# A state-space mixer's recurrence, from eight-step blocks to one scan instruction in a rotating frame

## The chip, the cores and the metric

The kernel runs on one core of one Trainium2 chip. The metric is the device time of one execution in microseconds (us). Engines are named as in the profile: PE (TensorE matmul), PEld (its weight load), DVE (VectorE), ACT (ScalarE), POOL (GpSimd) and SP (SyncE); a "q" behind a name is that engine's instruction queue (ACTq issues DMAs, for example). L1440 is line 1440 of the kernel before.

## What is computed

The program is two transformer-like blocks for one sequence of 256 tokens of width 1024 and a context of 256 tokens, all in float32. The part that the change touches is the state-space mixer of the second block's second layer. For each of two directions d, 64 groups and 64 states it runs a diagonal complex recurrence over the tokens:

```
step = exp(log_step);  mag = exp(lam_re * step)
a    = mag * (cos(lam_im * step) + i * sin(lam_im * step))
h_t  = a * h_(t-1) + B u_t          (h and B complex, u real)
y_t  = Re(C h_t) + D u_t
```

It runs first over the context (only its last state is kept), then over the latent sequence, which starts from that last state. The backward direction runs from the last token to the first.

## The kernel before, in words

**Chunks of four tokens.** Tables made once turn four tokens into one chunk: `ssm_build` (L1177) computes `a` from the parameters, then matrices that inject a chunk's four inputs into the state (tensor `ssm_m`), read a chunk's four outputs from the state (`ssm_g`), and hold the direct path inside a chunk (`ssm_t`); all go to DRAM. So 256 tokens are 64 chunks, and the recurrence over chunks has the factor a^4. States lie on 128 partitions; each partition holds 32 "pairs" x 2 directions x (real, imaginary) x 64 chunks.

**The recurrence before** is done in blocks of 8 chunks. `ssm_local` (L1425) walks the 8 places of a block, all blocks at once: for each of 7 steps two products of the previous place with a^4 (L1440) and two sums (L1443), each instruction over half of 8 pairs, 128 elements per partition. One call covers 8 pairs, so four calls cover the context and four the latent sequence; of each four, group g = 1 runs on GpSimd (`SSM_POOL`, `CTX_POOL`), the others on VectorE. `ssm_carry` (L1456 to L1464) then runs over the 8 blocks with a^32, four instructions of 128 elements for each of 7 steps. In the latent part `ssm_apply` (L1467 to L1481) adds the carried state, times a table of powers of a^4 (`spw`, from DRAM), to every place of every block: five instructions for each of 8 quarters q and each direction, most of the backward ones on GpSimd.

**The order of the stage.** `ssm_ctx` (L1484) normalises the context, multiplies it by the input weights (L1508), injects (L1408), runs the blocks and leaves `last`. It is called inside the dense expert layer ahead of it (`peer_dense`, L1049), so its instructions lie between those of that layer's last blocks (matmuls L777, splits L308 and L315). `ssm_mixer` (L1535) then normalises x, multiplies (lines 335 to 338), transposes into `suT`, injects all 32 pairs, runs blocks and carries, calls `fill` (modulation matmuls L796 to L806, weights `ada_w_t`), and goes q by q through apply, readout matmuls (L1596 with `ssm_t`, L1598 with `ssm_g`) and a Gelu (L1599). After that y is transposed and split (L1615, L1616) and the output matmuls follow.

**What sets the order.** The kernel is written in a framework that orders each engine's instructions by its own estimate of times; a lower priority (`c.low()`) is given to `ssm_build` and to the sparse expert branch. On the chip every engine and queue runs its list in that fixed order. Tiles come from pools with a number of buffers (`bufs`); a write to a buffer waits for the last reader of what was there. The weights `w` (1 MB tiles, L64) all go through one pool of 5 buffers and SP's queue, in program order. `ssm_build`'s tiles lie in the pool `sb`; when it is closed, the pools of the sparse branch and of the next norm take its space (L1672 to L1690), so these wait for `ssm_build`'s last store.

Of the kernel before, what the change touches and what calls it, by code (L numbers as in the profile page):

```python
# [41 lines left out]
SSM_POOL = (1,)  # L42
CTX_POOL = (1,)
APPLY_V = (0,)
# [1132 lines left out]
def ssm_build(c, pool, sb):  # L1177

    nc, I, tc = c.nc, c.I, c.tc
    A1, A2, B1, B2 = (pool.tile([P, 32, 2, 2], F32, name=n) for n in ("A1", "A2", "B1", "B2"))  # L1180
    pd = c.dram.tile([P, 1024], F32, name="ssm_p")
# [51 lines left out]
    pw = sb.tile([P, 5, 2, W], F32, name="pw")  # L1233
    tt(pw[:, 1, 0], mag, hs, ALU.mult)
    tt(pw[:, 1, 1], mag, sn, ALU.mult)
    ar, ai = pw[:, 1, 0], pw[:, 1, 1]
# [17 lines left out]
    def cmul(ore, oim, xr, xi, yr, yi, w1, w2):  # L1254
        tt(w1, xr, yr, ALU.mult)
        tt(w2, xi, yi, ALU.mult)
        tt(ore, w1, w2, ALU.subtract)
        tt(w1, xr, yi, ALU.mult)
        tt(w2, xi, yr, ALU.mult)
        tt(oim, w1, w2, ALU.add)  # L1260

    for n in (2, 3, 4):
        cmul(pw[:, n, 0], pw[:, n, 1], pw[:, n - 1, 0], pw[:, n - 1, 1], ar, ai, t1, t2)

    pt = sb.tile([P, 32, 2, 2, 8], F32, name="pt")
    nc.gpsimd.memset(pt[:, :, :, :, 0:1], 0.0)
    cur = pw[:, 4]
    for n in range(1, 9):
        if n > 1:
            nx = sb.tile([P, 2, W], F32, tag="pn", name="pn", bufs=2)  # L1270
            cmul(nx[:, 0], nx[:, 1], cur[:, 0], cur[:, 1], pw[:, 4, 0], pw[:, 4, 1], t1, t2)
            cur = nx
        srcs = [cur[:, j].rearrange("p (d q) -> p q d", d=2) for j in range(2)]
        if n < 8:
            for j in range(2):
                nc.scalar.copy(pt[:, :, :, j, n], srcs[j])
        if n in (1, 8):
            X1, X2 = (A1, A2) if n == 1 else (B1, B2)
            for r in range(2):
                nc.scalar.copy(X1[:, :, :, r], srcs[0])  # L1280
                nc.scalar.mul(X2[:, :, :, r], srcs[1], 1.0 - 2.0 * r)
    nc.scalar.dma_start(pd, pt.rearrange("p a d r n -> p (a d r n)"))
# [114 lines left out]
    return dict(a4=(A1, A2), a32=(B1, B2), powers=pd, m=md, g=gd, t=td)  # L1397


def ssm_inject(c, uT, Sx, mats, g, first=0):  # L1400


    for q in range(4 * g, 4 * g + 4):
        m = mats(q).rearrange("p (a j m) -> p a j m", a=2, j=4)
        ps = c.ps()
        for a in range(2):
            for j in range(4):
                c.nc.tensor.matmul(  # L1408
                    ps[:, (a * 4 + j) * 64 : (a * 4 + j + 1) * 64], m[:, a, j, :], uT[:, 2 * q + a, :], start=True, stop=True
                )  # L1410
        i = 2 * q - first
        c.evac(Sx[:, i : i + 2].rearrange("p a d r j -> p (a d r j)"), ps, eng="a")
# [12 lines left out]
def ssm_local(c, eng, pool, A, Sx, p0, n, tag, first=0):  # L1425

    m = n // 2

    def at(h, j):
        return _view(Sx, (p0 - first + h * m) * 256 + j, [[256, m], [128 + 7 - 2 * j, 2], [64, 2], [8, 8]])

    def step(j, i):

        for h in range(2):
            a = [v[:, p0 + h * m : p0 + (h + 1) * m].unsqueeze(4).to_broadcast([P, m, 2, 2, 8]) for v in A]
            if i < 2:
                t[h][i] = pool.tile([P, m, 2, 2, 8], F32, tag=f"{tag}{i}{h}", name=f"sl{i}", bufs=1)
                eng.tensor_tensor(t[h][i], a[i], at(h, j - 1), ALU.mult)  # L1440
            else:
                v = t[h][0] if i == 2 else _view(t[h][1], 8, [[32, m], [16, 2], [-8, 2], [1, 8]])
                eng.tensor_tensor(at(h, j), at(h, j), v, ALU.add)  # L1443

    t = [[None, None], [None, None]]
    for j in range(1, 8):
        for i in range(4):
            step(j, i)


def block_view(t, s):

    return _view(t, s, [[32, 32], [16 + 7 - 2 * s, 2], [8, 2]])


def ssm_carry(c, pool, B, e, before, after):  # L1456

    nc = c.nc
    t1 = pool.tile([P, 32, 2, 2], F32, tag="st1", name="st1")
    t2 = pool.tile([P, 32, 2, 2], F32, tag="st2", name="st2")  # L1460
# [6 lines left out]
def ssm_apply(eng, pool, pw, C, Sx, H, p0, n, d, tag):  # L1467

    shp = [P, n, 2, 8, 7]
    ps = slice(p0, p0 + n)  # L1470
    t1 = pool.tile(shp, F32, tag=tag + "1", name="sa1", bufs=1)
    t2 = pool.tile(shp, F32, tag=tag + "2", name="sa2", bufs=1)
    cb = C[:, ps, d].rearrange("p q r b -> p q (r b)").unsqueeze(3).to_broadcast([P, n, 16, 7])
    for r, t in enumerate((t1, t2)):
        power = _view(pw, p0 * 32 + d * 16 + r * 8 + (1 if d == 0 else 7), [[32, n], [0, 16], [1 - 2 * d, 7]])
        eng.tensor_tensor(t.rearrange("p q r b j -> p q (r b) j"), cb, power, ALU.mult)
# [443 lines left out]
```

## Time and profile before

| what | us |
|---|---|
| median of 3 runs | 3650.92 (3642.49 to 3659.8) |
| the profiled execution's own time | 3635.85 |
| its span | 3634.1 |
| PE busy | 3284.0 (90%) |
| DVE busy | 2640.1 (73%) |
| ACT busy | 1402.9 (39%) |
| POOL busy | 1338.2 (37%) |

The span runs from the first to the last instruction; the profiled execution's own time is 1.75 us longer. Busy shares are averages over stages with different limits, so the stages have to be looked at one by one. The state-space stage lies at 2445 to 2683 us; the set-up with `ssm_build` at 0 to 342 us. A duration of an instruction reaches a little into the next one on its engine, so a sum of durations can be larger than the time they took.

### The profile page before, as it was taken

The page shows a single profiled execution, that of the slowest core. Times are in us where ns is not written, and L with a number is a line of the kernel's source. Part 1 is how long each engine was busy: PE and PEld are TensorE (multiplying, and loading weights), DVE is VectorE, ACT ScalarE, POOL GpSimd, SP SyncE. Part 2 cuts the span into 40 slices and gives each one's busy share as a digit, 9 for nine tenths or more (in the row PEclk, how much of TensorE's full clock was granted, in tenths as well). Part 3 has the DMA queues.
Part 4 walks back from the last instruction along what each step waited for, and adds up shares of the span by engine and source line. Part 5 has one row for each costly group of instructions (what it writes and reads, how often), then busy time and mean ns, then how long its engine had stood idle before and what let it go on. Part 6 is the DMA issues. An engine that isn't in the chain of part 4 may idle for free.

```text
span 3634.1 us, 49746 instructions
## 1 busy us (share of the span) xinstructions
PE 3284.0 (90%) x18136; PEld 2665.8 (73%) x18136; DVE 2640.1 (73%) x5276; ACT 1402.9 (39%) x2586; POOL 1338.2 (37%) x1021
## 2 busy tenths in 40 slices
PE   6996987999889988879999999997589999999998
PEld 4775563747437756678899999976477988999987
DVE  5676986555655568878988888859968987555555
ACT  3553222011310023237444544442133475544454
POOL 0000244444334447448544444414444374001000
PEclk9997998999899999999999999998799999999999
DMA  8875778899588988586998888853554466555553
GB/s 304 288 246 185 280 254 312 336 343 338 211 315 333 355 325 277 178 275 206 357 342 329 338 335 330 336 197 109 199 197 174 163 192 238 209 209 209 209 203 116
DMA packets 280485, 940.44 MB, mean 259 GB/s; under 512 B 22944, under 2 KB 136880, under 8 KB 209200
## 3 DMA queue, kind: packets, MB, share of 16 engines
q1 hardware_dynamic: 142560, 608.22, 46.0%
q0 software_dynamic: 77184, 281.05, 21.2%
q10 hardware_dynamic: 60496, 47.99, 4.0%
q8 instruction: 142, 2.33, 0.2%
q14 instruction: 103, 0.84, 0.1%
HBM read 870.60 MB, written 66.58 MB: 258 GB/s over the span
## 4 chain that ended last, share of the span: by engine, by line
PE 57%; DVE 21%; DMA 13%; issue 4%; POOL 3%; ACT 2%; ACTq 1%; DVEq 0%; POOLq 0%; SPq 0%
PE bank L777 18%; PE bank L350 6%; PE bank L349 6%; PE bank L348 6%; DMA gat<-peer_u_rows,idx 5%; DMA gat<-peer_v_rows,idx 5%; PE bank L364 4%; PE bank L357 4%; DVE spl L315 2%; DVE sl L1440 2%; PE bank L909 2%; POOL o L1102 2%; PE bank L1105 1%; PE bank L337 1%; PE bank L335 1%
## 5 line engine op out<-in xcount | busy, mean ns | idle before, releaser
L315 DVE TENSOR_TENSOR spl<-w,sph 128x1024 fp32r<-128x1024 f32 x552 | 701.9, 1273 | 344.0 <-ACT sph L308 341.8
L308 ACT CAST sph<-w 128x1024 fp32r<-128x1024 f32 x632 | 661.9, 1049 | 558.9 <-PE bank L349 372.6
L350 PE MATMUL bank<-hs,spl 128*128 128x256 f32 x2048 | 582.5, 284 | 6.7 <-DVE spl L315 6.7
L348 PE MATMUL bank<-hs,sph 128*128 128x256 f32 x2048 | 581.0, 284 | 2.0 <-DVE mod L806 1.8
L349 PE MATMUL bank<-hs,sph 128*128 128x256 f32 x2048 | 581.0, 284 | 0.0
L1015 DVE CUSTOM_DVE_ANT_0 gat<-gat,htok 128x1024 f32<-128x1024 f32 x256 | 331.7, 1303 | 177.5 <-DMA gat<-peer_u_rows,idx 154.9
L1027 DVE SCALAR_TENSOR_TENSOR pacc<-gat,act,pacc 128x1024 f32<-128x1024 f32 x256 | 333.8, 1304 | 149.9 <-DMA gat<-peer_v_rows,idx 134.4
L348 PEld LDWEIGHTS bank<-hs,sph 128*128 128x128 f32 x2048 | 392.5, 192 | 11.6 <-ACT sph L308 1.9
L350 PEld LDWEIGHTS bank<-hs,spl 128*128 128x128 f32 x2048 | 392.7, 192 | 10.5 <-DVE spl L315 9.3
L349 PEld LDWEIGHTS bank<-hs,sph 128*128 128x128 f32 x2048 | 392.6, 192 | 8.3 <-issue 0.5
L315 POOL TENSOR_TENSOR spl<-w,sph 128x1024 fp32r<-128x1024 f32 x80 | 201.4, 2518 | 453.5 <-ACT sph L308 436.3
L364 PE MATMUL bank<-hT,w 128*128 128x256 f32 x1472 | 328.6, 384 | 14.1 <-DVE cv L509 8.4
L364 PEld LDWEIGHTS bank<-hT,w 128*128 128x128 f32 x1472 | 283.3, 193 | 64.9 <-issue 11.6
L777 PE MATMUL bank<-sph,wsl 128*128 128x512 f32 x1024 | 318.6, 392 | 2.3 <-DVE wsl L315 2.2
L1000 POOL DMA_INDIRECT gat<-peer_v_rows,idx x176 | 214.2, 1217 | 286.5 <-PE bank L357 61.2
L777 PE MATMUL bank<-spl,wsh 128*128 128x512 f32 x1024 | 319.4, 393 | 0.1
L777 PE MATMUL bank<-sph,wsh 128*128 128x512 f32 x1024 | 307.5, 394 | 2.4 <-ACT wsh L308 2.4
L1000 POOL DMA_INDIRECT gat<-peer_u_rows,idx x176 | 219.1, 1245 | 227.5 <-DVE act L1015 77.9
L357 PE MATMUL bank<-w,hT 128*128 128x512 f32 x576 | 255.6, 603 | 2.2 <-ACT sg L432 2.2
L777 PEld LDWEIGHTS bank<-sph,wsl 128*128 128x128 f32 x1024 | 192.2, 188 | 45.3 <-DVE wsl L315 2.6
L777 PEld LDWEIGHTS bank<-spl,wsh 128*128 128x128 f32 x1024 | 189.8, 188 | 39.8 <-DVE spl L315 0.3
L357 PEld LDWEIGHTS bank<-w,hT 128*128 128x128 f32 x576 | 110.7, 194 | 135.9 <-issue 132.0
(444 smaller groups left out, 5730.3 us busy)
## 6 DMA issues: line engine op xcount, KB each, us to landing
w<-peer_u_t SPq DMA_DIRECT2D x128, 1024.0 KB, 5.6
w<-peer_v_t SPq DMA_DIRECT2D x128, 1024.0 KB, 5.1
w<-ada_w_t SPq DMA_DIRECT2D x48, 1024.0 KB, 6.7
w<-wq_t SPq DMA_DIRECT2D x32, 1024.0 KB, 5.4
w<-w_in_t SPq DMA_DIRECT2D x32, 1024.0 KB, 7.9
gspill<-gstg SPq DMA_DIRECT2D x32, 896.0 KB, 4.6
gq<-gspill SPq DMA_DIRECT2D x28, 1024.0 KB, 6.2
w<-wqk SPq DMA_DIRECT2D x24, 1024.0 KB, 5.3
```

Source lines behind the costliest of these rows:

```text
L308: nc.scalar.copy(hi, src)
L315: eng.tensor_tensor(lo, src, hi.bitcast(F32), ALU.subtract)
L348: mm(ps, wh[:, ks], hh[:, k, :], start=k == 0, stop=False)
L349: mm(ps, wh[:, ks], hl[:, k, :], start=False, stop=False)
L350: mm(ps, wl[:, ks], hh[:, k, :], start=False, stop=k == KD - 1)
L357: m = self.nc.tensor.matmul(outs[t], hT[:, k, t * P : (t + 1) * P], w[k], start=k == 0, stop=k == KD - 1)
L364: m = self.nc.tensor.matmul(ps, block[:, k * P : (k + 1) * P], hT[:, k, :], start=k == 0, stop=k == KD - 1)
L777: c.nc.tensor.matmul(acc[t][cc], a[:, ts_], b[:, cc * 512 : (cc + 1) * 512], start=first and j == 0, stop=last and j == 2,)
L909: nc.tensor.matmul(ps[:, b * P : (b + 1) * P], wv[:, kt, k * P : (k + 1) * P], ks[:, kt, :], start=kt == 0, stop=kt == 1,)
L1000: g = nc.gpsimd.indirect_dma_start(out=gt, out_offset=None, in_=tab, in_offset=bass.IndirectOffsetOnAxis(ap=idx[:, t, s : s + 1], axis=0))
L1015: use = nc.vector.tensor_tensor_reduce(out=gt, in0=gt, in1=h[:, t, :], scale=1.0, scalar=0.0, op0=ALU.mult, op1=ALU.add, accum_out=act[:, ...
L1027: use = nc.vector.scalar_tensor_tensor(acc, gt, act[:, t, s : s + 1], acc, ALU.mult, ALU.add)
```

## The change

The state is turned by the phase of a^4: with a^4 = m e^(i theta), the turned state e^(-i n theta) h_n obeys a recurrence with the real factor m, which VectorE's `tensor_tensor_scan` runs over all chunks of several pairs in one instruction, separately for the real and the imaginary part. A decay table `dec` holds m everywhere and 0 at each pair's first chunk, so that one scan goes over 4 or 8 pairs. Afterwards the state is turned back.

- `ssm_build`: the powers of a up to a^32 (L1254 to L1282: 60 instructions of 64 elements on VectorE, 22 copies on ACT, one store) go. In their place come a normalisation of (cos, sin), a squaring chain on GpSimd (7 times 5 instructions of 64 elements), m and a^4 for all pairs, and 8 phase tables of 4 pairs each, on GpSimd: 2 memsets and 6 doubling levels of 6 instructions, with 8, 16, 32, 64, 128 and 256 elements. Each table (512 KB) is stored to DRAM by a DMA on ACT's queue; the table's buffer is single.
- `ssm_ctx`: eight steps of 4 pairs in place of four of 8. Each injects, loads its phase table (GpSimd's queue, 2 buffers), makes `dec` (two ACT copies, one GpSimd memset, one buffer), turns, scans, and copies the last chunk and its phase out (ACT); the turning back is done once at the end for the last chunk alone. The buffers of the injection weights `cw` go from 4 to 3.
- `ssm_mixer`: four groups of 8 pairs. Groups 0 to 2 are injected first, then `fill` follows, then group by group: phase tables (two DMAs on ACT's queue, 2 buffers), turn, add the start state, scan, turn back into `H` (2 buffers), and readout of two q. Group 3 is injected inside group 0's turn, when its buffer comes free; its weights are then asked for after `ada_w_t` and `ssm_t`. The apply and the carries go. GpSimd has no arithmetic left here.

The diff, cut to its core:

```diff
-SSM_POOL = (1,)
-CTX_POOL = (1,)
-APPLY_V = (0,)
...
 def ssm_build(c, pool, sb):
...
-    for n in (2, 3, 4):
-        cmul(pw[:, n, 0], pw[:, n, 1], pw[:, n - 1, 0], pw[:, n - 1, 1], ar, ai, t1, t2)
...
+    square(lv[:, 1], hs, sn)
+    square(lv[:, 0], lv[:, 1, 0], lv[:, 1, 1])
+    for l in range(1, 6):
+        square(lv[:, l], lv[:, l - 1, 0], lv[:, l - 1, 1])
...
+    def phases(k):
...
+        for l in range(6):
+            L = 1 << l
+            src = [_view(ph, cs * 512, [[320 - L, 2], [64, 4], [1, L]]) for cs in range(2)]
+            dst = [_view(ph, cs * 512 + L, [[320 - 3 * L, 2], [64, 4], [1, L]]) for cs in range(2)]
+            m = [_view(lv, l * 2 * W + cs * W + 4 * k, [[32, 2], [1, 4], [0, L]]) for cs in range(2)]
+            wv = w[:, :, :, :L]
+            for cs in range(2):
+                gp.tensor_tensor(dst[cs], src[0], m[cs], ALU.mult)
+                gp.tensor_tensor(wv, src[1], m[1 - cs], ALU.mult)
+                gp.tensor_tensor(dst[cs], dst[cs], wv, ALU.add if cs else ALU.subtract)
+        nc.scalar.dma_start(pd[k], ph.rearrange("p s d a n -> p (s d a n)"))
...
+def ssm_decay(c, pool, m4, p0, n):
+
+    dec = pool.tile([P, 2, n, 64], F32, tag="dec", name="dec")
+    for d in range(2):
+        c.nc.scalar.copy(dec[:, d], m4[:, p0 : p0 + n, d].unsqueeze(2).to_broadcast([P, n, 64]))
+    c.nc.gpsimd.memset(_view(dec, 0, [[n * 64 + 63, 2], [64, n]]), 0.0)
+    return dec
+
+
+def ssm_turn(nc, pool, ph, S, n):
+
+    w1, w2 = (pool.tile([P, 2, 2, n * 64], F32, tag=f"sw{i}", name=f"sw{i}") for i in range(2))
+    cs, si = (_view(ph, i * n * 128, [[n * 64, 2], [0, 2], [1, n * 64]]) for i in range(2))
+    nc.vector.tensor_tensor(w1, S.rearrange("p d r a j -> p d r (a j)"), cs, ALU.mult)
+    nc.vector.tensor_tensor(w2, _view(S, n * 64, [[n * 128, 2], [-n * 64, 2], [1, n * 64]]), si, ALU.mult)
+    return w1, w2
+
+
+def ssm_scan(c, pool, ph, dec, S, n, ini=None):
...
+    w1, w2 = ssm_turn(nc, pool, ph, S, n)
+    flat = S.rearrange("p d r a j -> p d r (a j)")
+    for r in range(2):
+        nc.vector.tensor_tensor(flat[:, :, r], w1[:, :, r], w2[:, :, r], ALU.subtract if r else ALU.add)
+    if ini is not None:
+        o = edge(S, n, False)
+        nc.vector.tensor_tensor(o, o, ini.rearrange("p a d r -> p d r a"), ALU.add)
+    N = n * 64
+    for d in range(2):
+        for r in range(2):
+            s = _view(S, (d * 2 + r) * N + d * (N - 1), [[1 - 2 * d, N]])
+            f = _view(dec, d * N + d * (N - 1), [[1 - 2 * d, N]])
+            nc.vector.tensor_tensor_scan(s, f, s, 0.0, ALU.mult, ALU.add)
...
 def ssm_mixer(c, mats, modT, x, last, fill, gate):
...
+            Sg = {g: inject(g) for g in range(3)}
+            fill(sy)
...
+            for g in range(4):
+                gs = slice(8 * g, 8 * g + 8)
+                ph = sy.tile([P, 4, 8, 64], F32, tag="ph", name="ph", bufs=2)
+                for h in range(2):
+                    nc.scalar.dma_start(
+                        ph[:, :, 4 * h : 4 * h + 4], mats["phase"][2 * g + h].rearrange("p (s a n) -> p s a n", s=4, a=4)
+                    )
+                S_ = Sg.pop(g)
+                ssm_scan(c, sy, ph, ssm_decay(c, sy, mats["m4"], 8 * g, 8), S_, 8, ini[:, gs])
+
+                w1, w2 = ssm_turn(nc, sy, ph, S_, 8)
+                if g == 0:
+                    Sg[3] = inject(3)
+                H = sy.tile([P, 2, 2, 8, 64], F32, tag="Hx", name="Hx", bufs=2)
+                nc.scalar.copy(edge(H, 8, False), last[:, gs].rearrange("p a d r -> p d r a"))
                 for d in range(2):
...
+                    for r in range(2):
+                        o, i = (slice(1, 64), slice(0, 63)) if d == 0 else (slice(0, 63), slice(1, 64))
+                        v1, v2 = (w[:, d, r].rearrange("p (a j) -> p a j", a=8)[:, :, i] for w in (w1, w2))
+                        nc.vector.tensor_tensor(H[:, d, r, :, o], v1, v2, ALU.add if r else ALU.subtract)
+                for q in (2 * g, 2 * g + 1):
...
```

## Rows read from the trace of the kernel before

**Rows 1.** Stretches of the span: us, busy time (count) by engine, clock, DMA share, GB/s

```profile
core 0: us, PE busy (x) PEld busy (x) DVE busy (x) ACT busy (x) POOL busy (x), PEclk, DMA share, GB/s
0.00:342.00 342.00, 263.15 (x1618) 208.92 (x1618) 223.02 (x631) 164.61 (x439) 8.54 (x15) 0.91 0.78 272
2445.00:2683.00 238.00, 164.47 (x1161) 143.71 (x1161) 222.74 (x484) 52.59 (x86) 126.35 (x161) 0.84 0.46 165
```

**Rows 2.** Chain of work, 2445 to 2683 us: shares of the 238 us by line

```profile
by line: DVE sl L1440 28.0%; DVE cSx L1443 14.6%; DVE Sx L1443 13.3%; DVE sa L1476 7.7%; PE bank L1598 4.5%; DVE spl L315 4.0%; DVE sa L1477 3.0%; DVE Hx L1481 2.8%; DVE sa L1478 2.3%; issue 2.2%; DVE st L1461 1.9%; DVE st L1463 1.8%; DVE s
```

**Rows 3.** Chain of work in order of time, 2440 to 2690 us: start us, us, what

```profile
2449.10 0.73 DVE sl L1440 x2
...
2583.21 2.30 DVE sl L1440 x4
...
2603.48 1.18 DVE sl L1440 x4
...
2667.64 0.97 DVE Hx L1481
2668.66 1.09 PE bank L1598 x8
...
2680.88 0.87 PE bank L1598 x8
...
2683.15 2.18 DVE y L1616 x4
```

**Rows 4.** DVE's groups, 2449 to 2675 us: count | busy us, mean ns | idle before

```profile
L1443 DVE TENSOR_TENSOR cSx<-cSx,sl 128x128 f32<-128x128 f32 x84 | 37.9, 486 | 1.0
L1476 DVE TENSOR_TENSOR sa<-sC,spw 128x448 f32<-128x448 f32 x18 | 21.8, 1248 | 0.0
L1461 DVE TENSOR_TENSOR st<-B,sC 128x128 f32<-128x128 f32 x7 | 2.8, 393 | 0.2
```

**Rows 5.** Single lines by form: count, ns min/median/max, first and last start, form

```profile
L486 DVE TENSOR_TENSOR_SCAN zf<-ones,lf x1: 670/670/670, 484.1 to 484.1; 4x256 f32<-4x256 f32 x1
...
L1305 DVE TENSOR_TENSOR w<-pb,pa x48: 402/424/432, 51.3 to 321.8; 128x256 f32<-128x256 f32 x48
...
L315 DVE TENSOR_TENSOR spl<-w,sph x552: 1164/1225/3757, 96.4 to 3614.6; 128x1024 fp32r<-128x1024 f32 x184
...
L315 POOL TENSOR_TENSOR spl<-w,sph x80: 2345/2403/3373, 1311.4 to 3467.2; 128x1024 fp32r<-128x1024 f32 x80
...
L315 POOL TENSOR_TENSOR wsl<-pw,wsh x31: 725/740/11582, 1721.6 to 3605.5; 128x256 fp32r<-128x256 f32 x31
...
L1440 POOL TENSOR_TENSOR sl<-A,Sx x28: 512/617/10272, 2560.1 to 2599.8; 128x128 f32<-128x128 f32 x28
```

**Rows 6.** SP's queue: start us, us, what (in groups), and DMA rate of a stretch

```profile
2558.53 19.26 SPq L64 DMA_DIRECT2D w<-ada_w_t  x8
2578.32 32.30 SPq L64 DMA_DIRECT2D w<-ssm_t  x2
2611.64 50.66 SPq L64 DMA_DIRECT2D w<-ssm_g  x8
...
2575.00:2580.00 5.00, 2.91 (x24) 1.39 (x24) 4.90 (x11) 0.89 (x2) 5.00 (x10) 1.00 1.01 428
```

**Rows 7.** Chain of work at the set-up's end, 255 to 360 us: start us, us, what

```profile
266.30 7.26 DMA ssm_t<-ts
...
338.19 3.11 DMA ssm_t<-ts
...
342.03 5.49 PE bank L251 x6
```

**Rows 8.** Set-up: two of DVE's groups, lines by form, the old power table's store

```profile
L1309 DVE TENSOR_TENSOR pb<-w,w 128x256 f32<-128x256 f32 x64 | 26.9, 421 | 11.1 <-ACT mt L1320 9.9
L315 DVE TENSOR_TENSOR spl<-w,sph 128x1024 fp32r<-128x1024 f32 x27 | 32.8, 1221 | 16.3 <-ACT sph L308 16.2
...
L1196 DVE TENSOR_TENSOR s<-pn,pw x24: 205/221/229, 70.0 to 107.0; 128x64 f32<-128x64 f32 x24
...
L1229 ACT ACTIVATE sn<-s x1: 256/256/256, 42.2 to 42.2; 128x64 f32<-128x64 f32 x1
...
DMA to landing us min/median/max: 9.4/9.4/9.4
```

**Rows 9.** Chain of work, 0 to 345 us: shares by line

```profile
by line: PE bank L909 11.0%; PE bank L796 6.5%; ACTq L1360 6.5%; PE bank L335 6.3%; PE bank L338 6.3%; PE bank L337 6.2%; DMA wqk<-mst 5.0%; DMA xc<-ctx 4.5%; issue 3.2%; DMA ssm_t<-ts 3.0%; PE bank L1376 3.0%; DVE ts L1386 2.7%; PE bank L8
```

More of the change, by code (lines that the diff above doesn't have):

```diff
@@ L1232, in ssm_build @@
     nc.vector.tensor_scalar(hs, hs, -2.0, 1.0, ALU.mult, ALU.add)
[L1233 to L1236, printed above, removed]
+    ar, ai = small("ar"), small("ai")
+    tt(ar, mag, hs, ALU.mult)
+    tt(ai, mag, sn, ALU.mult)
     den, am1 = small("den"), small("am1")
@@ L1267, in ssm_build @@
[L1267 to L1281, printed above, removed]
@@ L1282, in ssm_build, with square @@
[L1282 removed]
+    gp = nc.gpsimd
+    tt(t1, hs, hs, ALU.mult)
+    tt(t2, sn, sn, ALU.mult)
+    tt(t1, t1, t2, ALU.add)
+    nc.vector.tensor_scalar(t1, t1, -0.5, 1.5, ALU.mult, ALU.add)
+    tt(hs, hs, t1, ALU.mult)
+    tt(sn, sn, t1, ALU.mult)
+    lv = sb.tile([P, 6, 2, W], F32, name="lv")
+    g1, g2 = phi, k
+    def square(o, cs, si):
+        gp.tensor_tensor(g1, cs, cs, ALU.mult)
+        gp.tensor_tensor(g2, si, si, ALU.mult)
+        gp.tensor_tensor(o[:, 0], g1, g2, ALU.subtract)
+        gp.tensor_tensor(g1, cs, si, ALU.mult)
+        gp.tensor_tensor(o[:, 1], g1, g1, ALU.add)
@@ L1284, in ssm_build @@
+    for k in range(8):
+        phases(k)
     mt = sb.tile([P, NP, 2, 2, 4, 2, 16], F32, name="mt")
@@ L1396, in ssm_build, with ssm_inject @@
         nc.scalar.dma_start(td[:, q * NP * P : (q + 1) * NP * P], ts_.rearrange("p a t m -> p (a t m)"))
-    return dict(a4=(A1, A2), a32=(B1, B2), powers=pd, m=md, g=gd, t=td)
-def ssm_inject(c, uT, Sx, mats, g, first=0):
-    for q in range(4 * g, 4 * g + 4):
+    return dict(a4=(A1, A2), m4=M4, phase=pd, m=md, g=gd, t=td)
+def ssm_inject(c, uT, S, mats, p0, n):
+    for i in range(0, n, 2):
+        q = (p0 + i) // 2
         m = mats(q).rearrange("p (a j m) -> p a j m", a=2, j=4)
@@ L1418, in _view @@
     return bass.AP(t.tensor, t.offset + off, [list(ap[0])] + [list(d) for d in dims])
[L1425 to L1448, printed above, removed]
@@ L1467, in ssm_apply, with edge @@
[L1467 to L1476, printed above, removed]
-    eng.tensor_tensor(t1[:, :, 0], t1[:, :, 0], t2[:, :, 1], ALU.subtract)
-    eng.tensor_tensor(t1[:, :, 1], t1[:, :, 1], t2[:, :, 0], ALU.add)
-    hv, sv = (t[:, ps, d].rearrange("p q r (b j) -> p q r b j", b=8) for t in (H, Sx))
-    o, i = (slice(1, 8), slice(0, 7)) if d == 0 else (slice(0, 7), slice(1, 8))
-    eng.tensor_tensor(hv[:, :, :, :, o], t1, sv[:, :, :, :, i], ALU.add)
+def edge(S, n, last):
+    i = 63 if last else 0
+    return _view(S, i, [[2 * n * 64 + 63 - 2 * i, 2], [n * 64, 2], [64, n]])
@@ L1583, in ssm_mixer @@
+            nc.vector.tensor_tensor(ini, ini, _view(t2, 1, [[4, 32], [2, 2], [-1, 2]]), ALU.add)
+            y = sz.tile([64, 4, D], F32, name="sy")
             yv = y.rearrange("p t (q m) -> p q t m", m=32)
             tm = c.w(mats["t"], 32)
[L1585 to L1601 removed]
```

138 lines of the change are left out of this document (60 added, 78 removed).

## The prediction

> **What bounds the kernel now.** I read the busy shares by stretch first, then the chain of waits inside the stretches that the change touches, then single lines by form. PE is busy for 90% of the whole span, but not where the change works: between 2445 and 2683 us DVE is busy for 222.7 of 238 us and PE for 164.5, at a granted clock of 0.84 on average [rows 1]. The chain of that stretch is DVE's: the reader is to see that L1440 and L1443, the block steps, hold 55.9% of it, the apply lines L1476 to L1481 another 15.8% [rows 2]. In order of time the chain enters DVE at 2449 us, stays there until the last apply at 2667.6, goes over the readout matmuls L1598 for 13 us, and enters the split of y at 2683.15 [rows 3]. So here VectorE's time is time of the kernel, one to one, until something else is late. The set-up is mixed: from 0 to 342 us no engine is full (PE 263, DVE 223, ACT 165, POOL 8.5 us) [rows 1], but its end hangs on `ssm_build`: the last store of `ssm_t` lands, and only then the rows for the next norm start (L251 at 342.0) [rows 7]. A delay of `ssm_build` is therefore a delay of everything.
>
> **What goes.** The shares of the chain that the change removes are 28.0 + 14.6 + 13.3 (block steps) + 7.7 + 3.0 + 2.8 + 2.3 (apply) + 1.9 + 1.8 (carries) = 75.4% of 238 us = 179.5 us. L1462 and L1464 are cut off in that row; they have as many instructions as L1461 and I count them like it, 1.9% each: 9 us. Together 188 us of the path [rows 2]. The busy sums of the groups say the same size: four groups of 84 block-step instructions, near 38 us each, the apply 21.8 us in its first line, the carries 2.8 us per seven instructions [rows 4].
>
> **What comes, on VectorE.** A product or sum of 256 elements takes 0.42 us and one of 1024 takes 1.22 [rows 5]: 1.04 ns per element and 0.155 us fixed. That gives 0.29 us at 128 elements, which is what four block steps need on the chain without GpSimd (1.18 us for four) [rows 3], so I use it as time on the path: 0.69 us at 512, 2.29 at 2048. The scan is in the trace, on 4 partitions: 0.67 us for 256 elements [rows 5]. At 512 it lies between 0.94 (256 more at the sum's rate) and 1.34 (twice as long); I take 1.18, the same fixed part with two sum-steps per element, because that rate fits the row itself.
> - Context, 8 steps: two products of 1024, two sums of 512, four scans of 256: 2.44 + 1.38 + 2.68 = 6.5 us; times 8 is 52.
> - Latent, 4 groups: four products of 2048, two sums of 1024, one small sum, four scans of 512, four sums of 504: 9.16 + 2.44 + 0.2 + 4.72 + 2.76 = 19.3 us; times 4 is 77.
> - The context's last turn and the start state: seven of 128 elements, 2 us.
>
> Together 131 us (127 to 134 by the scan's bounds).
>
> **What lies beside it.** GpSimd loses its block steps and applies. While they ran, DVE's own steps took 2.30 us for four instead of 1.18 [rows 3]; that is inside the 188 us and is not counted again. The decay copies on ACT (about 0.6 us each, with ACT busy for 53 of 238 us [rows 1]) and the small memset hide behind the turn of the same group (2.4 to 4.6 us on DVE), as the one buffer comes free when the scans before end; if ACT is held up, the scan waits for it, and all of DVE's list behind it.
>
> **The end of the stage.** Before, the last q were read out behind the last apply in 13 us [rows 3]. Now two q (40 matmuls) follow the last turn: eight take 0.87 us [rows 3], so 4.4 us, or about twice that at half clock. I take 6 us less.
>
> **What is late next.** PE's work stays: 164 us at clock 0.84 [rows 1], perhaps 150 at full clock, and 150 is also about what DVE will need (222 - 188 + 131 = 165, part of it beside other work). Second, the weights: between the third injection and the first readout SP's queue now brings eight tiles of `ada_w_t`, two of `ssm_t`, two of `ssm_m` and one of `ssm_g`, 13 MB, besides 1 MB of phases per group. At the best rate seen, 428 GB/s [rows 6], that is 32 us, at 300 GB/s 46. DVE comes to the third `H` after 54 us, and its buffer is free only when the first group has been read out. The lower bound for these waits is 0, the upper some 30 us (all 14 MB at 300 GB/s, with no cover in the first 19-us group); I take 10, nearer to the low end, because eight tiles of `ada_w_t` were issued in 19 us [rows 6].
>
> State-space stage: -188 + 131 - 6 + 10 = **-53 us**, bounds -69 (127, no waits, -8) and -24 (134, 30 of waits, no gain at the end).
>
> **The set-up.** Gone: 60 VectorE instructions of 64 elements at 0.22 us [rows 8], 13 us, and 22 copies on ACT; VectorE gets about 15 small ones back. GpSimd gets 35 small squarings and 8 x 36 products. From 0.73 us at 256 elements and 2.40 at 1024 on GpSimd [rows 5]: 2.17 ns per element and 0.17 fixed. The six sizes of a table sum to 2.1 us, times six 12.7, with some 0.08 between dependent ones 15.6 us. The store of 512 KB landed in 9.4 us [rows 8], and the single buffer waits for that: 25 us a table, 200 us for eight. From about 60 us (squarings behind the sine, which runs at 42.2 [rows 8]) they end near 260, before 338 [rows 7]: hidden. GpSimd's 128-element products took 0.62 us at the median beside DVE, where the fit says 0.45, and the first one 10 us [rows 5]; by these the tables end near 320, still hidden.
>
> GpSimd's operands at the small levels lie 256 bytes apart. The Trainium skill (GPSIMD Engine Reference, section 7) has strided reads of more than 8 bytes cost half as much again per element; the row of strided products (0.51 us at best where the fit says 0.45) shows less. By the page the eight tables would take an estimated 26 us more, which moves the sum by nothing and only brings the late rival below nearer.
>
> What isn't hidden is DVE beside GpSimd: 192 products of 256 elements (L1305 to L1309, 27 us per 64) and 27 splits (33 us) [rows 8], 114 us, run at up to twice their time while GpSimd computes [rows 3], 125 of some 280 us: at most +51 us of DVE work, in a stretch where DVE idles for 119 us. About a quarter of that I put on the path, +12, against 9 us gained early: **+3 us** (-10 to +50).
>
> **Sum.** -53 + 3 = -50 us against the profiled execution's own 3635.85, so 3586 there. The median of the runs is 15 us higher, 3650.9; for runs like those I predict **3600 us**. About 0.5%, 18 us, is what a measurement of this kernel can tell from no change.
>
> **Rivals.**
> - *The readout is fed too slowly.* PE and the weights set the latent part's end, and DVE waits for `H`: waits of 30 to 35 us in place of 10. For it: the 13 MB above. Against it: DMA idle at times before (0.46 of the stretch [rows 1]). -53 + 22 + 3: about 3623.
> - *GpSimd slows VectorE in the set-up.* All of the 51 us lands on the path, because DVE's list stands still at its slow instructions: -53 + 51: about 3649, no change. For it: 2.30 against 1.18 us. Against it: DVE idle time there. The Trainium skill (GPSIMD Engine Reference, section 8) says that GpSimd shares its SBUF interfaces with VectorE, in contention with instructions that have two SBUF inputs, as all of these do; the trace agrees.
> - *GpSimd's tables hold ACT, slower than before.* The eight stores stand in ACT's queue at places chosen from the framework's estimate. If GpSimd is later than that, ACT waits, and behind it the casts and PSUM copies that DVE and PE need. From 6 us per table on (8 x 6 = 48) the gain is gone; at 10 us per table it is -53 + 80 + 3: about 3681. For it: ACT's queue already holds 6.5% of the set-up's chain at `ssm_build`'s stores (L1360) [rows 9]. Against it: 25 us per table lie in a stretch of 340.
> - *The scan stage is tighter.* No waits and full overlap: -69 - 8, about 3574.
>
> **How the numbers follow.** Forecast 0.60, slow feed 0.15, set-up contention 0.10, tables holding ACT 0.08, tighter 0.07. Faster by over 0.5% (below 3633) holds the forecast, the slow feed and the tighter case: 0.82. Within 0.5%: 0.11, the contention and a little of its neighbours. Slower: 0.07. The forecast alone runs from 3580 to 3620. The range reaches from 3568 to 3643: it takes in the slow feed and the tighter case and leaves out most of the last two in 10.
>
> **What would show it.** Right: in the new profile the stage from the context's injection to the split of y lasts 180 to 190 us instead of 238; scans near 0.67 and 1.18 us, turns near 2.3; the first norm row (L251 before) still starts near 342 us. Wrong: scans of 512 well over 1.4 us, or turns slower than 2.4, make the 131 too small; idle DVE time before `H` or the turn, ended by a DMA or a readout, shows the feed; a start of the norm row later than 350 us, with ACT waiting for GpSimd or DVE's L1305 lines over 0.6 us, shows the set-up rivals. If the stage shrinks and the norm rows are in place but the end isn't earlier, a later stage has taken the time back, and the prediction has no term for that.

## The result, and the profile after

The changed kernel takes **3588.26 us** (median of 4 runs, 3574.18 to 3596.69); beside it the kernel before took 3646.70 (4 runs, 3639.18 to 3659.8). The ratio is 0.9837, with a 95% interval of 0.9809 to 0.9865: 1.6% faster. A second comparison gave 3583.34 against 3650.61, 0.9817 (0.9789 to 0.9844). The profiled execution after took 3596.56 us with a span of 3594.5. It is one of the slower of its four, and the profiled one of before (3635.85 us, span 3634.1) was faster than all four beside it, so the two traces differ by only 39.6 us where the medians differ by 58. What follows accounts for the 39.6 first.

The stretches that answer to [rows 1], same columns:

```profile
0.00:342.00 342.00, 270.62 (x1688) 215.43 (x1689) 246.94 (x606) 164.53 (x427) 148.07 (x357) 0.93 0.81 283
2457.00:2644.00 187.00, 161.22 (x1097) 145.31 (x1096) 147.28 (x173) 55.71 (x117) 13.67 (x30) 0.84 0.67 236
```

VectorE is busy for 147 of 187 us, where it was busy for 222.7 of 238; PE's work (161 us) and its mean clock (0.84) are what they were. GpSimd has gone over to the set-up. VectorE's list in time order (start us, us, what, and in brackets the idle time before it):

```profile
2457.67 1.23 DVE L1461 TENSOR_TENSOR sw<-cSx,cph 128x1024 f32<-128x1024 f32 x1 [4.32 <-ACT cSx L156]
...
2534.24 1.39 DVE L1553 STREAM_TRANSPOSE suT<-half 128x512 f32<-128x512 f32 x2 [5.53 <-ACT half L156]
2547.75 2.29 DVE L1461 TENSOR_TENSOR sw<-Sx,ph 128x2048 f32<-128x2048 f32 x1 [12.12 <-DMA ph<-ssm_p]
...
2612.98 2.46 DVE L1598 TENSOR_TENSOR Hx<-sw,sw 128x504 f32<-128x504 f32 x4 [10.88 <-ACT Hx L1593]
...
2631.96 2.46 DVE L1598 TENSOR_TENSOR Hx<-sw,sw 128x504 f32<-128x504 f32 x4
...
2644.18 4.17 DVE L1628 TENSOR_TENSOR y<-bank,y 128x256 fp32r<-128x256 f32 x8 [7.49 <-ACT y L1627]
```

From the first context turn to the split of y it is 186.5 us; in [rows 3] it was 234.05, from 2449.10 to 2683.15. Three waits stand in it that the old stage did not have: 5.53 us before the last transposes of the input, 12.12 before the first latent turn and 10.88 before the third `H`.

**Where the 39.6 us come from.** SP's queue gives a mark ahead of the stage that all kernels share, the load of the mixer's input weights (`ssm_w_in_t`: 2399.16 before, 2398.19 after). Up to it: -1.0 us. From it to VectorE's first block step or turn: 49.9 before, 59.5 after, +9.5. The stage: -47.5. From the split of y to the end: 950.9 and 950.3, -0.6. Sum -39.6. In all fourteen profiles of this study that last part lies between 949.1 and 953.7, so what stands ahead of the split of y makes the differences; this is why the table below measures from the load to the split. (The load itself lies anywhere between 2381.6 and 2402.8 us, so executions also differ by what lies ahead of it.)

The stage between its two marks, before and after, columns as in [rows 1]:

```profile
2449.10:2683.15 234.05, 160.52 (x1130) 139.89 (x1129) 221.60 (x483) 51.57 (x84) 125.46 (x160) 0.83 0.45 163
```

```profile
2457.67:2644.18 186.51, 160.73 (x1095) 144.86 (x1093) 147.28 (x173) 55.28 (x116) 13.31 (x30) 0.84 0.66 235
```

VectorE's busy time fell by 74.3 us (221.6 to 147.3) and its idle time rose by 26.8 (12.4 to 39.2): together -47.5.

VectorE's groups between 2457 and 2636 us (count | busy us, mean ns | idle before):

```profile
L1481 DVE TENSOR_TENSOR_SCAN cSx<-dec,cSx 128x256 f32<-128x256 f32 x32 | 19.5, 671 | 0.0
L1461 DVE TENSOR_TENSOR sw<-Sx,ph 128x2048 f32<-128x2048 f32 x8 | 18.3, 2292 | 12.5 <-DMA ph<-ssm_p 12.1
L1481 DVE TENSOR_TENSOR_SCAN Sx<-dec,Sx 128x512 f32<-128x512 f32 x16 | 18.3, 1205 | 0.4
L1462 DVE TENSOR_TENSOR sw<-Sx,ph 128x2048 f32<-128x2048 f32 x8 | 18.3, 2284 | 0.0
L1472 DVE TENSOR_TENSOR cSx<-sw,sw 128x512 f32<-128x512 f32 x16 | 10.3, 685 | 0.0
L1598 DVE TENSOR_TENSOR Hx<-sw,sw 128x504 f32<-128x504 f32 x16 | 9.9, 678 | 11.0 <-ACT Hx L1593 10.9
L1462 DVE TENSOR_TENSOR sw<-cSx,cph 128x1024 f32<-128x1024 f32 x8 | 9.7, 1218 | 0.0
L1461 DVE TENSOR_TENSOR sw<-cSx,cph 128x1024 f32<-128x1024 f32 x8 | 9.7, 1206 | 4.4 <-ACT cSx L156 4.3
...
L1472 DVE TENSOR_TENSOR Sx<-sw,sw 128x1024 f32<-128x1024 f32 x8 | 9.4, 1221 | 0.1
```

The context is 9.7 + 9.7 + 10.3 + 19.5 = 49.2 us; the latent groups 18.3 + 18.3 + 9.4 + 18.3 + 9.9 and 0.9 of small sums = 75.1.

**Who holds the third H.** Its buffer is free when the first group has been read out. PE, and then ACT, of the changed kernel in time order:

```profile
2546.77 7.31 PE L1426 MATMUL bank<-suT,w 128*128 128x64 f32 x64
2554.01 1.92 PE L793 MATMUL bank<-w,sc 128*32 128x512 f32 x16
2566.29 1.86 PE L798 MATMUL bank<-sel,half 128*128 128x2 f32 x8 [10.36 <-ACT half L156]
...
2585.10 1.87 PE L798 MATMUL bank<-sel,half 128*128 128x2 f32 x8 [5.99 <-DVE Hx L1598]
2586.83 13.89 PE L1426 MATMUL bank<-suT,w 128*128 128x64 f32 x64
2600.65 0.69 PE L1605 MATMUL bank<-w,suT 128*64 128x128 f32 x2
```

```profile
2550.54 0.59 ACT L156 COPY Sx<-bank 128x512 f32<-128x512 f32 x1 [1.20 <-PE bank L1426]
2559.66 1.14 ACT L1452 COPY dec<-M 128x512 f32<-128x512 f32 x2 [8.53 <-DVE Sx L1481]
2560.70 1.06 ACT L156 COPY Sx<-bank 128x512 f32<-128x512 f32 x2
2564.13 1.48 ACTq L1583 DMA_DIRECT2D ph<-ssm_p  x2
2565.65 0.59 ACT L156 COPY half<-bank 128x512 f32<-128x512 f32 x1 [3.88 <-issue]
```

Read upwards from the readout (L1605, 2600.65): it stands behind the fourth injection (L1426), that behind the modulation (L793, L798), and the modulation waited 10.36 us for one ACT copy (`half`, 2565.65). That copy was ready to run since 2556. ACT stood at the decay copy L1452, whose only buffer the scans of group 0 were still reading, and then at the issue of the next phase load, whose buffer group 0 held until its turn back. ACT's list runs in order, so both waits became PE's: 3.9 us of it behind the phase issue, the rest behind the decay copy and the two copies that follow it. The 5.99 us at 2585.10 are the same once more, behind the issue of the fourth group's phases (ACT, 2583.21). PE waited for no weight between 2534 and 2601.

**The set-up after.** The line of `ssm_t`'s stores (count, ns min/median/max, first and last start), against [rows 7]:

```profile
L1414 ACTq DMA_DIRECT2D ssm_t<-ts x8: 326/338/582, 86.2 to 317.8; - x8
```

VectorE's products up to 345 us, against [rows 8]:

```profile
L1327 DVE TENSOR_TENSOR pb<-w,w 128x256 f32<-128x256 f32 x64 | 30.3, 473 | 9.1 <-ACT mt L1338 6.3 <-ACT gb L1338 0.8
L1326 DVE TENSOR_TENSOR w<-pb,pa 128x256 f32<-128x256 f32 x48 | 24.5, 511 | 0.0
L1323 DVE TENSOR_TENSOR w<-pb,pa 128x256 f32<-128x256 f32 x48 | 21.5, 449 | 0.9
```

GpSimd in time order, the fills that begin the second and the eighth table:

```profile
85.03 0.15 POOL L1286 MEMSET ph<- 128x8 f32 x2 [7.64 <-DMA ssm_p<-ph]
...
246.88 0.15 POOL L1286 MEMSET ph<- 128x8 f32 x2 [8.41 <-DMA ssm_p<-ph]
```

The last store of `ssm_t` is issued 20.4 us earlier than before (338.2), and in SP's queue the next stage's first `ada_w_t` load 16.5 us earlier (357.32, in the old trace 373.86). The products cost 0.45 to 0.51 us instead of 0.42. The two fills are 161.85 us apart, 27 us per table.

### The profile page after: what moved, and what is told of

Its sections match the earlier page's. It is cut to its first block, busy times and chain, and to the rows that moved or that the text cites. A ratio compares the mean times of both kernels' runs of the same rounds, so it can differ in the third digit from the quotient of the medians.

```text
span 3594.5 us, 49686 instructions
## 1 busy us (share of the span) xinstructions
PE 3294.9 (92%) x18136; PEld 2679.8 (75%) x18136; DVE 2577.2 (72%) x4922; ACT 1408.9 (39%) x2606; POOL 1359.2 (38%) x1232
## 5 line engine op out<-in xcount | busy, mean ns | idle before, releaser
L345 PEld LDWEIGHTS bank<-hs,sph 128*128 128x128 f32 x2048 | 392.6, 192 | 12.1 <-ACT sph L305 1.9
```

Of the source, the lines that this page charges most:

```text
L345: mm(ps, wh[:, ks], hh[:, k, :], start=k == 0, stop=False)
```

## The experiments

One table first; the waits are VectorE's, "load to split" runs from the `ssm_w_in_t` load to the split of y in the profiled execution, "first readout" is counted from the first context turn.

| kernel | load to split | stage | wait before first latent turn | before third H | median us | ratio to before |
|---|---|---|---|---|---|---|
| before | 284.0 | 234.1 | - | - | 3646.7 | 1 |
| changed | 246.0 | 186.5 | 12.1 | 10.9 | 3588.3 | 0.9837 |
| after_again | 246.3 | 186.8 | 12.6 | 10.7 | 3583.3 | 0.9817 |
| ph_early | 233.9 | 174.4 | 4.8 | 7.3 | 3578.1 | 0.9803 |
| act_free | 240.1 | 180.6 | 9.8 | 7.3 | 3582.4 | 0.9806 |
| early_free | 231.3 | 171.8 | 4.8 | 8.9 | 3574.6 | 0.9793 |
| fill_late | 225.5 | 166.0 | 4.8 | 0 | 3571.9 | 0.9816 |
| fill_late0 | 225.1 | 165.6 | 4.8 | 0 | 3567.3 | 0.9800 |
| scan_twice | 269.8 | 210.3 | 5.4 | 0 | 3607.6 | 0.9903 |
| no_tables | 239.3 | 179.8 | 5.7 | 10.4 | 3587.6 | 0.9849 |
| cw4 | 237.6 | 194.7 | 5.5 | 3.2 | 3584.0 | 0.9839 |
| late_cw4 | 236.0 | 193.1 | 5.5 | 0 | 3578.1 | 0.9824 |

Ratios have intervals of about 0.002 to 0.003 to either side, so neighbours in the last column are not told apart; the trace's "load to split" is the finer measure. The medians come from several comparisons whose kernel before stood at 3643 to 3651, so only the ratios compare across them.

**after_again**: the changed kernel, unedited.

> The changed kernel once more, as the measure for the others of this call. If the difference between the two profiled executions (39 us) and that between the medians (58 us) are draws of one distribution, the ratio comes out between 0.982 and 0.987 again, and the stage from the first context turn to the split of y lasts 185 to 189 us, with VectorE idle for about 12 us before the first turn of the latent groups and about 11 us before the H of the third group.

Ratio 0.9817, just below the range; stage and both waits as expected. The stage repeats within 0.3 us in these two executions, while whole runs scatter over some 20 us.

**ph_early**

```
 uT = sx.tile([P, 32, 64], F32, name="suT")
+phs = {g: phase(g) for g in range(2)}   # the loads of L1583, tile from pool sx
```

> The phase tables of the first two latent groups are asked for at the head of the mixer, from a pool that is open before the norm, on ACT's queue as before. Theory (the load is late and nothing else): the 12.1 us for which VectorE stood before the first latent turn fall to about 5, because the last of the first group's four injected copies ended at 2540.4 us, 7 us before that turn; the whole tail moves by 7 us, ratio about 0.002 below the changed kernel's. Rival (PE and the readout set the end): the 7 us come back as a longer wait before H of the third group, 18 us instead of 11, and the time is that of the changed kernel within 2 us.

The wait fell to 4.8 us, now for the injected copy, and the wait before H did not grow but fell to 7.3. The stage lost 12.4 us, more than the 7 expected: with group 0 ready earlier, ACT's waits for its scans end earlier too, and PE's wait of 10.36 us for the copy is 2.83 here. The rival is out. Whole time 5 us less, within the scatter.

**act_free**

```
-dec = pool.tile([P, 2, n, 64], F32, tag="dec", name="dec")
+dec = pool.tile([P, 2, n, 64], F32, tag="dec", name="dec", bufs=2 if n == 8 else 1)
-nc.scalar.dma_start(ph[...], mats["phase"][...])
+nc.gpsimd.dma_start(ph[...], mats["phase"][...])
```

> The decay tile of the latent groups gets a second buffer and the phase loads of the latent groups go to GpSimd's DMA queue instead of ACT's. Theory (ACT's list stands behind the scans): ACT idled 8.5 and 6.6 us before its decay copies until the scans before had ended, and 3.9 us at the issue of a phase load; behind it stood the copies that the filled-in modulation on PE needs, so PE idled some 17 us between 2548 and 2600 and the first readout started at 2603. Freed, the first readout starts 8 us or more earlier, the 10.9 us before H of the third group fall to under 3, and the kernel gains 6 to 10 us (0.2 to 0.3%). Rival (the weights on SP's queue are late): PE still waits, for ssm_m and ssm_g, the wait before H stays near 11 us and the time does not move.

Half right. The stage lost 6.1 us; the wait before H fell to 7.3, not under 3; the first readout came 137.2 us behind the first turn instead of 143.0. ACT, and then PE, of this kernel in time order show why it was not more:

```profile
2562.10 1.14 ACT L1452 COPY dec<-M 128x512 f32<-128x512 f32 x2 [4.42 <-DVE Sx L1481]
...
2581.03 1.14 ACT L1452 COPY dec<-M 128x512 f32<-128x512 f32 x2 [6.59 <-DVE Sx L1481]
```

```profile
2564.26 1.87 PE L798 MATMUL bank<-sel,half 128*128 128x2 f32 x8 [3.56 <-ACT half L156]
...
2577.54 1.94 PE L793 MATMUL bank<-w,sc 128*32 128x512 f32 x8 [0.99 <-DMA w<-ada_w_t]
2582.71 1.87 PE L798 MATMUL bank<-sel,half 128*128 128x2 f32 x8 [3.24 <-ACT half L156]
```

PE's wait of 10.36 us is 3.56 now, so the theory holds for that. But the second buffer only moved ACT's wait on by one group: the decay copy of group 2 still stands ahead of the modulation's copies and waits for the scans of group 0.

The other half of the edit shows that ACT's queue was not what made the first phase load late. The first loads in the changed kernel, and then here on GpSimd's queue:

```profile
2534.58 0.60 ACTq L1583 DMA_DIRECT2D ph<-ssm_p  x1
```

```profile
2539.65 3.01 POOL L1583 DMA_DIRECT2D ph<-ssm_p  x4 [19.25 <-ACT half L156]
```

That is 76.9 and 77.5 us behind the first context turn. GpSimd's queue stood for 19.25 us until ACT's copies of the input product (`half`) were done. By the kernel's text the pool of the phase tables opens only when the norm's pool, which feeds that product, is closed; ph_early, which asks from an earlier pool, is free of it. VectorE's wait fell here only from 12.1 to 9.8.

**early_free**: both edits.

> Both edits: phase tables asked for at the head of the mixer (on GpSimd's queue) and two decay buffers. If both theories hold the gains add: 13 to 17 us less than the changed kernel (0.4 to 0.5%), stage of 170 to 174 us. If PE or the weights set the end, less than 5 us, with VectorE's idle time moved to before H of the later groups.

The stage lost 15.0 us (172, in the range expected), the time 8.8 us by the medians of one comparison. Alone the two edits took 12.4 and 6.1, so they share some 3.5 us. The wait before H stayed at 8.9, and now the weights are behind it too (PE of early_free in time order):

```profile
2557.50 1.07 PE L793 MATMUL bank<-w,sc 128*32 128x512 f32 x8 [1.86 <-DMA w<-ada_w_t]
2561.51 1.94 PE L793 MATMUL bank<-w,sc 128*32 128x512 f32 x8 [2.94 <-DMA w<-ada_w_t]
...
2568.97 13.91 PE L1426 MATMUL bank<-suT,w 128*128 128x64 f32 x64 [2.95 <-DMA w<-ssm_m]
```

**fill_late and fill_late0**: early_free, and the modulation called later.

```
 Sg = {g: inject(g) for g in range(3)}
-fill(sy)
 ...
     nc.scalar.activation(yv[...], ..., AF.Gelu_apprx_tanh)
+if g == 1:      # fill_late0: if g == 0
+    fill(sy)
```

> Both edits of the run early_free, and the modulation of the next block (eight 1 MB tiles of ada_w_t on SP's queue and 64 matmuls) is called behind the readout of the second latent group instead of ahead of the first. Theory (the order of the weights is what is left): in early_free PE waited for ada_w_t and ssm_m between 2557 and 2569 us and the first readout started 131 us behind the first context turn; with ssm_t, ssm_m and ssm_g first it starts at 118 to 122, the 8.9 us before H of the third group fall to under 2, and the stage lasts 160 to 166 us instead of 172. Rival (the 8 MB only move): VectorE waits no longer before H, but PE reads out the last groups behind the modulation, the split of y comes as late as before and the stage lasts 170 to 175 us, the time that of early_free within 4 us.

> As fill_late, but the modulation is called behind the readout of the first latent group, not the second. Theory (what matters is only that ssm_t, ssm_m and ssm_g come ahead of the 8 MB): stage 165 to 168 us and the same time as fill_late within 3 us. Rival (its 8 MB come ahead of the weights of the second to fourth readout, which then wait): a wait before H of the third or fourth group of 4 to 10 us again, stage 170 to 176 us.

Both came as the theories said in what counts: no wait before H, stages of 166.0 and 165.6 us (the whole times, from two comparisons, lie 4.7 us apart). In both the fourth injection runs on behind the third, and the first readout comes 99.5 us behind the first turn (143.0 in the changed kernel, 130.7 in early_free), some 20 earlier than the theory of fill_late had it. The reason given is not shown alone: the edit moves the modulation's 8 MB and also its matmuls and its waits for ACT's copies from ahead of the readout. In early_free PE's waits for weights there make 7.8 us of the 31 that were gained at the first readout; no run separates the rest. PE of fill_late0 in time order:

```profile
2513.60 27.13 PE L1426 MATMUL bank<-suT,w 128*128 128x64 f32 x242
2540.66 0.43 PE L1608 MATMUL bank<-w,suT 128*64 128x128 f32 x2
```

The stretch of the fourth injection in fill_late0 and then in the changed kernel, columns as in [rows 1] (the granted clock is the last but two):

```profile
2533.00:2541.00 8.00, 8.00 (x73) 7.93 (x72) 7.86 (x7) 3.05 (x6) 1.64 (x3) 1.00 0.89 314
```

```profile
2587.00:2601.00 14.00, 14.00 (x66) 13.88 (x67) 13.86 (x13) 2.94 (x6) 0.13 (x1) 0.50 0.48 166
```

This is the version that beats both kernels in the trace: 225.1 us from load to split against 246.0. By the whole time it is 0.9800 (0.9776 to 0.9825) of before; the intervals of the changed kernel, around 0.9837 and 0.9817, overlap with that, and the two were not timed in one comparison. Its gain over the changed kernel is 21 us in the trace, 16 to 21 by the medians and 6 to 13 by the ratios. That the later modulation adds anything to early_free (0.9793) shows in the trace alone: 231.3 from load to split became 225.5 and 225.1, while the ratios are 0.9816 and 0.9800.

**scan_twice**

```
     nc.vector.tensor_tensor_scan(s, f, s, 0.0, ALU.mult, ALU.add)
+    nc.vector.tensor_tensor_scan(s, f, s, 0.0, ALU.mult, ALU.add)
```

> Every scan of the changed kernel is issued twice in a row (the second runs over the first one's output, so the recurrence is no longer the reference's). That is 32 context scans and 16 latent ones more on VectorE: 32 x 0.61 + 16 x 1.14 = 38 us by the profile of the changed kernel. Theory (VectorE's time in this stage is time of the kernel, one to one): 30 to 38 us more, at least the whole 20 us in the context part, where VectorE has no wait, and some of the latent share swallowed by the 11 us before H of the third group. Rival (since the change PE or the weights set the stage): less than 15 us more.

Between the two: the stage grew by 23.5 us over after_again's, the median by 19 to 24. The added scans are all there (VectorE's groups, L1482), and the waits are these (us in total, times, longest us):

```profile
L1482 DVE TENSOR_TENSOR_SCAN cSx<-dec,cSx 128x256 f32<-128x256 f32 x32 | 19.9, 666 | 0.0
...
L1482 DVE TENSOR_TENSOR_SCAN Sx<-dec,Sx 128x512 f32<-128x512 f32 x16 | 18.2, 1197 | 0.0
```

```profile
DVE y L1629 <- ACT y L1628: 10.1, 1, 10.1
...
DVE mod L803 <- PE bank L798: 6.4, 1, 6.4
DVE sw L1461 <- DMA ph<-ssm_p: 5.4, 1, 5.4
```

38.1 us of work went in. Against after_again the phase wait gave 7.2 us of it back, the wait before H 10.7 and the one for the last transpose 5.5; two others grew by 9.1. That makes 38.1 - 23.4 + 9.1 = 23.8. In the context part alone, where VectorE hardly waits, the eighth turn comes 74.9 us behind the first instead of 55.1: 19.8 us for the 18.6 added ahead of it. So VectorE's time is time of the kernel in the context, and in the latent groups only from the point where its waits are used up.

**no_tables, before_tables and before_small**: the set-up. In no_tables the products of a table are replaced by one fill; before_tables puts them into the kernel before; before_small is

```
 def cmul(ore, oim, xr, xi, yr, yi, w1, w2):
-    tt(w1, xr, yr, ALU.mult)
+    nc.gpsimd.tensor_tensor(w1, xr, yr, ALU.mult)
     ...
```

> The 288 products and sums that make the phase tables are left out of the set-up of the changed kernel; each table is filled with ones and stored as before (so the turns turn by nothing). Theory (the tables are hidden; contention costs about what VectorE's rows show, 10 us of busy time over 192 products, of which little is on the path): the set-up ends 0 to 6 us earlier and the time is that of the changed kernel within 8 us, ratio 0.980 to 0.983. Rival (contention with GpSimd is on the path to its full size): the products go back from 0.45 to 0.51 us to 0.42 and the first load of the next stage (ada_w_t, at 357 to 362 us) comes 10 us earlier or more, ratio 0.979 or below.

> The kernel before, with the products, sums, memsets and stores of eight phase tables added on GpSimd in its set-up and not used (multipliers of the same layout from its own table of powers; the squarings are left out). Theory (hidden, as forecast): ratio 0.999 to 1.004, the first ada_w_t load behind the set-up at 374 to 384 us. Rival (GpSimd's tables slow VectorE or hold ACT by what the forecast gave as its worse cases): 1.010 to 1.025, with the ada_w_t load 35 to 80 us late.

> The kernel before, with its 60 small products and sums of the powers of a (64 elements each) issued on GpSimd instead of VectorE; nothing else. In the changed kernel the last store of ssm_t was issued at 317.8 us instead of 338.2 and the first ada_w_t load behind the set-up at 357 to 369 instead of 374. Theory (those 60 instructions, 13 us, stood ahead of the products of the set-up on VectorE and on its path): the last store comes 8 to 20 us earlier than 338 here too, the ada_w_t load at 358 to 368 us, and the time is 5 to 12 us lower, ratio 0.9965 to 0.9985. Rival (the set-up gained by something else, the 22 ACT copies or the order of the lists): last store 335 to 342 us, ratio 0.999 to 1.002.

Without the tables the changed kernel is no faster: 3587.6 us, 0.9849 (0.9828 to 0.9870), its `ada_w_t` load at 365.5. The three large groups of products are back at 0.42 to 0.43 us, so it is GpSimd's work beside them that slows them; the end of the set-up gains nothing by it. With them the kernel before is no slower: 3641.6 against 3643.8, **1.0001** (0.9987 to 1.0015), the load at 377.7. The line of its stores and VectorE's products, as above:

```profile
L1417 ACTq DMA_DIRECT2D ssm_t<-ts x8: 326/332/341, 94.8 to 342.3; - x8
```

```profile
L1330 DVE TENSOR_TENSOR pb<-w,w 128x256 f32<-128x256 f32 x64 | 28.6, 448 | 22.7 <-ACT mt L1341 21.2 <-ACT gb L1341 0.2
L1329 DVE TENSOR_TENSOR w<-pb,pa 128x256 f32<-128x256 f32 x48 | 22.6, 470 | 0.0
```

The products are slower here as well, and the last store and the load come some 4 us later than before; in the time that does not show (5 us either way by the interval). In before_small the last store came at 329.5 and the load at 364.3, 8.7 and 9.5 us early, which is about half of what the changed kernel gained there; but the first load of the experts' weights, at 1602.3, was no earlier than before (1599.5), and the time is 0.9989 (0.9968 to 1.0010): whether it reaches the end is not settled by this run. The rest of the 20.4 us at the store stays open.

no_tables also shows how far an edit shifts a stage that it does not touch: the lists' order comes from the framework's estimate, and its load to split is 239.3, 7 us under the changed kernel's, nearly all of it at the first latent turn (5.7 us of waiting for 12.1). That is as much as act_free gained, so the size of act_free's gain proves little by itself; its rows do.

**cw4 and late_cw4**: four weight buffers in the context (`bufs=4 if tag == "cw" else 2`), alone and on top of fill_late.

> The changed kernel with four buffers for the context's weight tiles, as the kernel before has, instead of three. From the last common loads of the expert stage (2384) the context's first block step came 64.4 us later in the kernel before and its first turn 73.9 us later in the changed one. Theory (the third buffer less makes the context's matmuls wait for weights): the first turn comes within 66 us of that load, and the time falls by 3 to 8 us. Rival (the order of the lists, in which PE does more of the experts first): 72 to 75 us again, and no difference in time, since PE is busy all through and what it does earlier it does not do later.

> All of fill_late (phase tables asked for at the head of the mixer, two decay buffers, the modulation behind the second latent group) and four weight buffers for the context. If the edits are independent: stage from the first context turn to the split of y 164 to 168 us, no wait of VectorE before H, 3566 to 3576 us, ratio 0.977 to 0.981. If the fourth buffer only shifts work to PE's list: the same as fill_late within 3 us.

In cw4 the first turn came 42.9 us behind the `ssm_w_in_t` load (59.5 in the changed kernel), so the +9.5 us at the stage's start go with that buffer. It is not a wait for weights, as the theory had it: between the load and the first block step or turn PE is busy all through in all three kernels (49.94 us with 210 matmuls before, 59.48 with 254 in the changed kernel, 42.92 with 180 in cw4). What differs is how many matmuls PE's list puts ahead. The stage got 8 us longer, the sum of both 8.4 us shorter, the time no different (3584.0). On top of fill_late the sum is 10.5 us longer than without. The start came earlier, as the theory of cw4 said; the gain in time did not come, as its rival said. In late_cw4 the edits are not independent: the short stage did not come. Whether its whole time is that of fill_late (0.9824 against 0.9816) the intervals do not tell.

## Why the prediction was right, and where it was not

3600 us was forecast, 3568 to 3643; 3588 came, for the reason given: VectorE's work in the stage is shorter, and the stage with it. That the number is so near is in part luck. VectorE's busy time fell by 74.3 us where -188 + 131 = -57 was forecast, and its idle time rose by 26.8 where 10 - 6 = 4 was: two errors of 17 and 23 us that nearly cancel.

- **What goes and what comes.** 131 us were forecast on VectorE: 52 + 77 + 2. The rows show 49.2 + 75.1 + 1.8 = 126. Scans 0.67 and 1.20 us (0.67 and 1.18 forecast), turns 2.29 and 2.28 (2.29). So 5 of the 17 us are new work that came out smaller. The other 12 went or grew shorter beside the 188 that were read off the chain; which instructions they are was not followed up.
- **The end of the stage**: 6 us less forecast. From the end of the last H (2634.4) to the split of y it is 9.8 us, against 14.5 from the end of the last apply in [rows 3] (2668.6): 4.8 less. The 4.4 us put on the last readout were too few: 40 matmuls show as 80 in the trace, and from the last `H` they take 10 us at full clock (2632.69 to 2643).
- **Waits: the step that was mis-sized.** 10 us forecast (0 to 30), 23.0 measured before the first latent turn and the third H, and 5.5 more before the last transposes. "Its buffer is free only when the first group has been read out" was right. But the prediction named the weights as the reason, for which PE did not wait there, and costed the decay copies at nothing because they "hide behind the turn of the same group". They do not delay VectorE, as it said; they stand in ACT's list ahead of other work, wait for VectorE's scans there, and so, with the phase issue behind them, held PE for 10.36 us. And the phases were counted as bytes beside the weights, not as a load that can be asked for only behind the input product: by ph_early that is 7.3 of the 12.1 us, the other 4.8 are a wait for the injected copy. ph_early, act_free and fill_late each take a share of the waits away: the late phases, ACT's list, and the modulation ahead of the readout. The shares overlap.
- **The readout is fed too slowly**, the rival with 30 to 35 us of waits and 3623: with 23.0 us the waits came out between it and the forecast. What kept the time down was the 17 us above.
- **The start of the stage** had no term: +9.5 us in the profiled pair, by PE's order (cw4).
- **The stage in sum**: -53 forecast, -47.5 from the first block step or turn to the split, -38.0 from the common load.
- **The set-up**: +3 forecast, earlier by 16.5 us at the `ada_w_t` load in this trace. In the eleven profiles of the changed kernel and its variants that load stands at 357 to 369 us, in the two of before and before_tables at 373.9 and 377.7. Contention was rightly small: the 192 products took 91.0 us instead of 80.8, 10 more, where up to 51 were allowed and 12 put on the path; before_tables shows that they cost no time that can be measured. The Trainium skill (GPSIMD Engine Reference, section 8) has GpSimd contend with VectorE where an instruction has two SBUF inputs; the trace agrees in kind, with 0.45 to 0.51 us for 0.42. Too small was the gain: the six norm rows of [rows 7] (L251, 342.03) start at 323.94, not "still near 342". (The very first norm row stood at 334.5 before, not at 342.)
- **The tables**: 25 us each forecast, 27.0 measured, the last begun at 246.88; hidden. That is 16 us more for eight, of which the causes are not separated. The 26 us put beside the forecast would need every operand element to lie apart; above the first doubling level 2 to 32 lie together. ACT's waits for GpSimd in the set-up are one of 8.7 us, so the rival of held tables is out.
- **The scan stage is tighter** (3574) would have needed no waits; fill_late0, with none before H and 4.8 us before the first turn, took 3567.
- **Medians.** The first `peer_u_t` load, at about 1590 us on average in the eleven profiles (1581 to 1600), stands at 1599.5 to 1603.0 in the three of the kernel before and its variants: some 12 us, which with the 38 make 50 of the 58 to 67 between the medians. What makes the 12 is not shown: in before_small the set-up ended 9.5 us earlier and that load did not move. The rest is within the scatter of single executions and stays open.

## What to carry to other kernels

When a busy engine is relieved, look at the in-order lists of the engines that serve it: a small copy that waits for a single buffer is free for its consumer, and may still hold everything behind it. Cost such an instruction by what stands behind it, not by its own consumer's slack. And when a stage gets shorter, look at the work and the bulk loads of a later stage that were put into it when it was long: here they stood ahead of what the stage itself waited for.

## What the hardware showed unexpectedly

PE's clock added to PE's waits. The fourth injection, 64 matmuls, took 13.89 us at a granted clock of 0.50 (1.2 of 2.4 GHz) behind PE's waits of 10.36 and 5.99 us, where the same 64 took 7.31 us at 2546.77, when PE had just been busy all through; in fill_late0, with no wait ahead, the clock there is 1.00. That is 6.6 us of the first readout's delay. In all eight profiles in which the modulation stands ahead of it, with waits of 2.6 to 6.2 us shortly before, the fourth injection took 13.9 us. A scan of 128x512 took 1.20 us, 1.8 times one of 128x256 (0.67), and no less when run a second time on the same data. GpSimd's first product in the set-up took 0.87 us, not the 10 that its first one took in the block steps [rows 5].
